# Sums of weight blocks of a retention layer kept in DRAM between two halves of the tokens

## Chip, cores and metric

One core of one Trainium2 chip runs the kernel. The metric is the device time of one execution in microseconds; the kernel before took 1784.6 us (median of 3 runs, 1781.79 to 1789.89).

## What is computed

A two-layer decoder trunk on 1024 tokens of width 1024, all in float32. The part that matters here is the first layer, retention with 4 heads:

```python
u = rms_norm(h, ret_norm_pre[i])
proj = u @ ret_w_in[i]
q, k, v, g = jnp.split(proj, [...], axis=-1)
...
o = retention_chunkwise(q, k, v)
...
o = merge_heads(o).astype(h.dtype) * jax.nn.silu(g)
y = o @ ret_w_out[i]
h = h + rms_norm(y, ret_norm_post[i])
```

For each head, `v` and the gate `g` are 512 columns wide. The second layer is stick-breaking attention with 8 heads, whose keys and values come from a shared projection of the first layer's output.

## The kernel before

**Halves and phases.** The tokens are worked in two halves of 512. `run` (L1179) goes through four phases: retention on the first half (A, t=0), retention on the second (A, t=1), attention on the first half (C, t=0), attention on the second (C, t=1). Weights don't stay on chip: every phase loads them again.

**Products.** A float32 product is made of three products of split operands: `split` (L270) has ScalarE copy the value to a shorter format (the high part) and VectorE subtract that from the value (the low part); `mm3` (L108) multiplies high by high, high by low and low by high. Weights pass through this each time they are loaded: a block of 128 x 512 (256 KB) lands in a `wraw` buffer (6 of them, L42), is split, and stands in a `whl` buffer (3 of them, each for a unit of two blocks).

**The value and gate products (`vg`, L466).** For every head but the first head of the first half, `v` and `g` are computed together by a scheme with seven half-size products in place of eight, at the price of sums of weight blocks. `order` (L524) names the products 1, 2, 5, 6, 3, 7, 4, each in two units `i`. `left(n, i)` (L473) prepares a unit in two blocks `c`: products 1, 2 and 4 take a weight block as it is; product 5 loads two blocks and adds them (L493) into a tile `S` (2 buffers, one for each `i`); product 6 loads one block and changes `S` in place by a subtraction (L496); product 3 loads one block and subtracts `S` from it in its `wraw` buffer (L499); product 7 loads one block and changes `S` in place again (L502). Then comes the split. A head loads 32 blocks. `get(at)` and `get(at + 1)` in `chunk` (L527) ask for the unit in use and the next one. A unit is 12 matmuls on TensorE.

**Heads and their surroundings.** The first head of the first half (u=0, t=0) computes `v` and `g` without this scheme. Between two `vg` stretches stand the query/key products of the next head and the output product of the last one, whose partial sums go to DRAM and back (`y_d`). In the second half `a_post` (L684) rebuilds the first half's residual in side steps (L706, L707, L715 and L716) spread over the heads.

**The order of the work.** All DMAs are issued on SP's queue (`dma`, L63); an issue waits on SP for what its transfer needs. The code only says which instruction needs which: in what order an engine or a queue takes its instructions is laid out beforehand by a planner, so instructions that are ready early can stand ahead of ones written before them. Buffers come free when their last reader is done, a DMA that reads them included.

**A relative of the change that exists already.** In the attention phases the sums of the value weights are made beside other work by `w_sums` (L783, called for t=0), stored to DRAM tiles `S_d` (L289), and loaded in `values` instead of the blocks.

Of the kernel before, what the change touches and what calls it, by code (L numbers as in the profile page):

```python
# [10 lines left out]
F32 = mybir.dt.float32  # L11
# [7 lines left out]
NH = 4  # L19
# [12 lines left out]
def trunk(ctx, tc, xT, wts, gains, trig, ident_in, cols, out):  # L32
# [13 lines left out]
    def S(tag, shape, dt=F32):  # L46
        cnt[0] += 1
        return sb.tile([128] + list(shape), dt, tag=tag, name=f"{tag}{cnt[0]}", bufs=BUFS[tag])

    def PS(tag):  # L50
        cnt[0] += 1
        return ps.tile([128, 512], F32, tag=tag, name=f"p{tag}{cnt[0]}", bufs=BUFS[tag])

    def DRAM(name, dt):
        return dr.tile([128, 1024], dt, tag=name, name=name)
# [4 lines left out]
    def f32(ap):  # L60
        return ap.bitcast(F32)

    def dma(dst, src, eng=nc.sync):  # L63
        eng.dma_start(dst.bitcast(F32), src.bitcast(F32))
# [43 lines left out]
    def mm3(p, lh, ll, rh, rl, start, stop, goes_on=False):  # L108

        kw = dict(skip_group_check=True) if goes_on else {}  # L110
        MM(p, lh, rh, start=start, stop=False, **kw)  # L111
        MM(p, lh, rl, start=False, stop=False, **kw)  # L112
        MM(p, ll, rh, start=False, stop=stop, **kw)  # L113
# [29 lines left out]
    def ahead(n, make):  # L143

        box = {}

        def get(u):
            if u < n and u not in box:
                box[u] = make(u)
            return box.get(u)  # L150
        return get
# [118 lines left out]
    def split(dst, src, scale=None):  # L270

        if scale is None:
            A_.activation(dst[0], src, AF.Copy)  # L273
            V.tensor_tensor(dst[1], src, f32(dst[0]), ALU.subtract)  # L274
        else:
            A_.activation(dst[0], src, AF.Copy, scale=scale)  # L276
            V.scalar_tensor_tensor(dst[1], src, scale, f32(dst[0]), ALU.mult, ALU.subtract)  # L277
# [6 lines left out]
    y_d = [[dr.tile([128, 512], F32, tag=f"y{t}{c}", name=f"y{t}{c}") for c in range(8)] for t in range(2)]  # L284
    h_d = [[DRAM(f"h{t}{c}", F32) for c in range(4)] for t in range(2)]
    k_d = [DRAM(f"k{h}", F32R) for h in range(8)]
    v_d = [[DRAM(f"v{p}{b}", F32R) for b in range(4)] for p in range(NPAIR)]
    T_d = [{n: [DRAM(f"T{t}{n}{i}", F32R) for i in range(2)] for n in (5, 6, 7, 4)} for t in range(2)]
    S_d = [{n: [dr.tile([128, 512], F32, tag=f"s{g}{n}{k}", name=f"s{g}{n}{k}") for k in range(4)]  # L289
# [132 lines left out]
    class AHead:  # L422
# [43 lines left out]
        def vg(self):  # L466


            X, base, h = self.X, self.base, self.h
            self.v, self.sg = [None] * 4, [None] * 4  # L470
            box = {"S": [None, None]}

            def left(n, i):  # L473

                w = S("whl", [2, 1024], F32R)
                if n == 5:
                    box["S"][i] = S("S", [1024])
                for c in range(2):
                    cl = slice(512 * c, 512 * c + 512)

                    def load(which, kk):
                        raw = S("wraw", [512])
                        dma(raw[:], wts[base + 4 + 4 * which + kk, :, cl])
                        return raw[:]

                    s = box["S"][i][:, cl] if box["S"][i] else None
                    if n == 1:
                        src = load(0, i)
                    elif n == 2:
                        src = load(0, 2 + i)  # L490
                    elif n == 5:
                        a, b, src = load(1, i), load(1, 2 + i), s
                        V.tensor_tensor(src, a, b, ALU.add)  # L493
                    elif n == 6:
                        a, src = load(0, i), s
                        V.tensor_tensor(src, src, a, ALU.subtract)  # L496
                    elif n == 3:
                        src = load(0, 2 + i)
                        V.tensor_tensor(src, src, s, ALU.subtract)  # L499
                    elif n == 7:  # L500
                        a, src = load(1, 2 + i), s
                        V.tensor_tensor(src, a, src, ALU.subtract)  # L502
                    else:
                        src = load(1, 2 + i)
                    split((w[:, 0, cl], w[:, 1, cl]), src)
                return w

            def right(n, kt, tb):
                tl = slice(128 * tb, 128 * tb + 128)
                if n in (1, 2, 3):  # L510
                    x, o = X.xh[kt + (0 if n == 1 else 4)], 0 if n == 3 else 256
                    return [x[:, l, o + 128 * tb:o + 128 * tb + 128] for l in range(2)]
                return [X.T[kt][{5: 0, 6: 1, 7: 2, 4: 3}[n]][:, l, tl] for l in range(2)]

            def copy(p):
                c = S("f2", [512])
                A_.activation(c[:], p[:], AF.Copy)
                return c

            def plus(c, p):  # L520
                V.tensor_tensor(c[:], p[:], c[:], ALU.add)
                return c[:]

            order = [(n, i) for n in (1, 2, 5, 6, 3, 7, 4) for i in range(2)]  # L524
            get = ahead(14, lambda at: left(*order[at]))

            def chunk(n, i, kk):  # L527
                if kk == 0:
                    at = order.index((n, i))
                    get(at)  # L530
                    get(at + 1)
                    box["w"] = get(at)
                    if i == 0:
                        first = {1: "ma", 2: "o", 5: "mb", 4: "mb"}.get(n)
                        if first:
                            box["p", n] = [PS(first), PS(first)]
                w, kt = box["w"], 2 * i + kk
                banks = box["p", {6: 1, 7: 1, 3: 5}.get(n, n)]
                first = n in (1, 2, 5, 4)
                for tb in range(2):  # L540
                    xh, xl = right(n, kt, tb)
                    cl = slice(512 * kk, 512 * kk + 512)
                    mm3(banks[tb][:], xh, xl, w[:, 0, cl], w[:, 1, cl], first and kt == 0, kt == 3, goes_on=not first)
                if kt < 3:
                    return
                for tb, p in enumerate(banks):
                    if n in (1, 5, 6, 7):
                        box[n, tb] = copy(p)
                    if n in (1, 5, 6):
                        pass  # L550
                    elif n == 2:
                        self.vput(2 + tb, plus(box[1, tb], p), cc[:, 4 * h + 2 + tb:4 * h + 3 + tb])
                    elif n == 3:
                        self.vput(tb, plus(box[6, tb], p), cc[:, 4 * h + tb:4 * h + tb + 1])
                    elif n == 7:
                        self.gput(tb, plus(box[5, tb], p))
                    else:
                        self.gput(2 + tb, plus(box[7, tb], p))

            return Chunks([lambda n=n, i=i, kk=kk: chunk(n, i, kk) for n, i in order for kk in range(2)], lambda: get(0))  # L560
# [781 lines left out]
```

## Time and profile before

| | us |
|---|---|
| median of 3 runs | 1784.6 |
| lowest and highest run | 1781.79, 1789.89 |
| the profiled execution | 1780.48 |
| its span, first to last instruction | 1778.8 |
| granted TensorE clock, mean | 0.994 |

| engine | busy us | share of the span |
|---|---|---|
| TensorE (PE) | 1719.9 | 97% |
| VectorE (DVE) | 1295.9 | 73% |
| ScalarE (ACT) | 873.0 | 49% |
| GpSimd (POOL) | 285.2 | 16% |

The profile is one execution. PEld is the loading of the stationary operand, which overlaps PE. Rows of the timeline give the start in us from the span's start, the duration, the engine, the line, the operation, the tiles as out<-in, and in brackets the idle time of the engine before it and what ended it. Rows of the waits give the total, the number of waits and the longest. Rows of the windows give, for a stretch of time, each engine's busy time with its count of instructions, the granted clock, the busy share of the 16 DMA engines and the GB/s. A matmul's end is modelled, so PE's busy time hides short pauses. The DMA queue of SP carries all data: 347.26 MB in the execution, 273.78 MB read from DRAM and 73.40 MB written, 57.3% of the engines' time.

### The profile page before, as it was taken

Reading aid. Unit: us, or ns where it says so; the run is one execution under the profiler, and the core shown is the slowest. Engines: PE = TensorE matmul, PEld = TensorE weight load, DVE = VectorE, ACT = ScalarE, POOL = GpSimd, SP = SyncE. Lnnn points to the kernel's source line nnn. Section 1 sums busy time; section 2 is a strip of 40 time slices with the busy share of each in tenths; the row PEclk is TensorE's granted clock in tenths of the full one; section 3 lists DMA queues with packets and bytes.
Section 4 is the critical chain, followed back from the end, with each engine's and each line's share of the span. In section 5 each row is a group of like instructions: output and inputs, shape, how many; then the busy total and the mean of one; then the engine's idle time right before and its main releaser. Section 6 shows DMA issues by size and latency. Waiting matters only on the chain. (4 is left out here: it accounts for less than half of the span.)

```text
span 1778.8 us, 24255 instructions
## 1 busy us (share of the span) xinstructions
PE 1719.9 (97%) x8036; PEld 1416.6 (80%) x8036; DVE 1295.9 (73%) x2131; ACT 873.0 (49%) x1630; POOL 285.2 (16%) x377
## 2 busy tenths in 40 slices
PE   8999999999999899999999999999999999999997
PEld 7888788778788787778777788888887888888776
DVE  7756767889867968597688767668887656757765
ACT  6435545455444535365555444545564444545541
POOL 0210412332304310202112100000200010000003
PEclk9999999999999999999999999999999999999998
DMA  5225465557436656275886888558683762552523
GB/s 191 84 101 196 154 237 172 201 184 272 161 135 208 210 167 214 92 264 188 289 297 225 307 300 292 202 189 283 239 294 109 237 212 97 169 187 95 196 78 118
DMA packets 182381, 348.80 MB, mean 196 GB/s; under 512 B 20336, under 2 KB 24560, under 8 KB 182256
## 3 DMA queue, kind: packets, MB, share of 16 engines
q1 hardware_dynamic: 182256, 347.26, 57.3%
q8 instruction: 63, 1.03, 0.2%
q14 instruction: 62, 0.51, 0.1%
HBM read 273.78 MB, written 73.40 MB: 195 GB/s over the span
## 5 line engine op out<-in xcount | busy, mean ns | idle before, releaser
L274 DVE TENSOR_TENSOR whl<-wraw,whl 128x512 fp32r<-128x512 f32 x368 | 257.7, 730 | 62.8 <-ACT whl L273 62.5
L273 ACT ACTIVATE whl<-wraw 128x512 fp32r<-128x512 f32 x368 | 216.7, 624 | 123.5 <-PE pmb L113 57.3
L276 ACT ACTIVATE whl<-wraw,gn 128x256 fp32r<-128x256 f32 (+1 forms) x240 | 133.5, 605 | 112.4 <-PE pmb L113 58.1
L277 DVE SCALAR_TENSOR_TENSOR whl<-wraw,gn,whl 128x256 fp32r<-128x256 f32 (+1 forms) x240 | 140.4, 625 | 51.1 <-ACT whl L276 47.8
L111 PE MATMUL pmb<-xh,whl 128*128 128x512 f32 x384 | 153.6, 400 | 1.5 <-DVE sg L988 1.4
L111 PE MATMUL pma<-xh,whl 128*128 128x512 f32 x384 | 153.4, 400 | 0.0
L113 PE MATMUL pma<-xh,whl 128*128 128x512 f32 x384 | 150.8, 393 | 0.0
L113 PE MATMUL pmb<-xh,whl 128*128 128x512 f32 x384 | 150.3, 391 | 0.0
L112 PE MATMUL pma<-xh,whl 128*128 128x512 f32 x384 | 150.1, 391 | 0.0
L112 PE MATMUL pmb<-xh,whl 128*128 128x512 f32 x384 | 150.1, 391 | 0.0
L1018 POOL TENSOR_SCALAR_AFFINE_SELECT sgn<-sgn 128x128 f32<-128x128 f32 x64 | 28.2, 441 | 666.4 <-ACT sgn L1013 612.8
L1020 DVE TENSOR_TENSOR_SCAN sgn<-sgn 128x128 f32<-128x128 f32 (+3 forms) x64 | 89.0, 1391 | 28.0 <-POOL sgn L1018 27.9
L273 ACT ACTIVATE AT<-pz 128x512 fp32r<-128x512 f32 (+1 forms) x96 | 46.6, 487 | 118.6 <-PE pz L1050 118.6
L111 PE MATMUL pmb<-oT,whl 128*128 128x512 f32 x240 | 96.7, 403 | 5.9 <-DVE sg L988 3.0
L113 PE MATMUL pmb<-oT,whl 128*128 128x512 f32 x240 | 95.1, 396 | 0.4 <-DVE whl L274 0.4
L274 DVE TENSOR_TENSOR AT<-pz,AT 128x512 fp32r<-128x512 f32 (+1 forms) x96 | 53.0, 554 | 58.2 <-ACT AT L273 57.9
L112 PE MATMUL pmb<-oT,whl 128*128 128x512 f32 x240 | 94.6, 394 | 0.0
L111 PEld LDWEIGHTS pmb<-xh,whl 128*128 128x128 f32 x384 | 72.6, 189 | 17.4 <-DVE sg L988 4.0
L113 PEld LDWEIGHTS pmb<-xh,whl 128*128 128x128 f32 x384 | 72.3, 188 | 15.9
L113 PEld LDWEIGHTS pma<-xh,whl 128*128 128x128 f32 x384 | 72.4, 188 | 15.6
L273 ACT ACTIVATE whl<-S 128x512 fp32r<-128x512 f32 x92 | 56.9, 630 | 56.7 <-DVE S L496 17.0
L112 PEld LDWEIGHTS pmb<-xh,whl 128*128 128x128 f32 x384 | 72.5, 189 | 13.5
(365 smaller groups left out, 4545.8 us busy)
## 6 DMA issues: line engine op xcount, KB each, us to landing
wraw<-in_wts_dram SPq DMA_DIRECT2D x632, 256.0 KB, 3.5
y<-f SPq DMA_DIRECT2D x120, 256.0 KB, 3.1
f<-y SPq DMA_DIRECT2D x88, 256.0 KB, 3.3
wraw<-s SPq DMA_DIRECT2D x48, 256.0 KB, 3.0
T<-AT SPq DMA_DIRECT2D x32, 256.0 KB, 3.0
sc<-T SPq DMA_DIRECT2D x16, 512.0 KB, 4.4
v<-v SPq DMA_DIRECT2D x16, 512.0 KB, 5.1
vo<-v SPq DMA_DIRECT2D x32, 256.0 KB, 2.9
```

Source lines behind the costliest of these rows:

```text
L111: MM(p, lh, rh, start=start, stop=False, **kw)
L112: MM(p, lh, rl, start=False, stop=False, **kw)
L113: MM(p, ll, rh, start=False, stop=stop, **kw)
L273: A_.activation(dst[0], src, AF.Copy)
L274: V.tensor_tensor(dst[1], src, f32(dst[0]), ALU.subtract)
L276: A_.activation(dst[0], src, AF.Copy, scale=scale)
L277: V.scalar_tensor_tensor(dst[1], src, scale, f32(dst[0]), ALU.mult, ALU.subtract)
L1018: G.affine_select(n[:, dg], n[:, dg], [[-1, 128]], ALU.is_gt, 1.0, base=0, channel_multiplier=1)
L1020: V.tensor_tensor_scan(n[:, :W][:, ::-1], n[:, :W][:, ::-1], n[:, :W][:, ::-1], 1.0, ALU.mult, ALU.bypass)
```

## The change

Heads 1, 2 and 3 of the first half store each block that they split for products 5, 6, 3 and 7 to new DRAM tiles `s_d`: 16 blocks a head. For products 5, 6 and 7 the stored block lies in `S`, for product 3 in the `wraw` buffer. In the second half these heads load the 16 blocks from there and split them; they make no sums and take no `S` tile. Products 1, 2 and 4 stay as they were, and so does the first head in the second half, which has no stored blocks (`h` is 0). The tiles of `s_d` for h=1 and product 7 (place 3 in the list) bear the names s130 and s131, which two tiles of `S_d` have as well.

```diff
@@ -284,6 +284,7 @@
     y_d = [[dr.tile([128, 512], F32, tag=f"y{t}{c}", name=f"y{t}{c}") for c in range(8)] for t in range(2)]
     h_d = [[DRAM(f"h{t}{c}", F32) for c in range(4)] for t in range(2)]
     k_d = [DRAM(f"k{h}", F32R) for h in range(8)]
+    s_d = [[[DRAM(f"s{h}{n}{i}", F32) for i in range(2)] for n in range(4)] for h in range(NH)]
     v_d = [[DRAM(f"v{p}{b}", F32R) for b in range(4)] for p in range(NPAIR)]
@@ -473,6 +474,14 @@
             def left(n, i):
 
                 w = S("whl", [2, 1024], F32R)
+                kept = s_d[h][(5, 6, 3, 7).index(n)][i] if n in (5, 6, 3, 7) and h else None
+                if kept is not None and self.t:
+                    for c in range(2):
+                        cl = slice(512 * c, 512 * c + 512)
+                        raw = S("wraw", [512])
+                        dma(raw[:], kept[:, cl])
+                        split((w[:, 0, cl], w[:, 1, cl]), raw[:])
+                    return w
                 if n == 5:
                     box["S"][i] = S("S", [1024])
                 for c in range(2):
@@ -503,6 +512,8 @@
                     else:
                         src = load(1, 2 + i)
                     split((w[:, 0, cl], w[:, 1, cl]), src)
+                    if kept is not None:
+                        dma(kept[:, cl], src)
                 return w
```

## The prediction

> **What bounds the kernel now.** I read the page first (busy time, then the DMA issues), then the table of windows over the stretches that the change touches, then the waits and the order of time inside one of them.
>
> ```profile
> span 1778.8 us, 24255 instructions
> PE 1719.9 (97%) x8036; PEld 1416.6 (80%) x8036; DVE 1295.9 (73%) x2131; ACT 873.0 (49%) x1630; POOL 285.2 (16%) x377
> wraw<-in_wts_dram SPq DMA_DIRECT2D x632, 256.0 KB, 3.5
> y<-f SPq DMA_DIRECT2D x120, 256.0 KB, 3.1
> f<-y SPq DMA_DIRECT2D x88, 256.0 KB, 3.3
> wraw<-s SPq DMA_DIRECT2D x48, 256.0 KB, 3.0
> S<-in_wts_dram SPq DMA_DIRECT2D x16, 256.0 KB, 5.3
> s<-S SPq DMA_DIRECT2D x16, 256.0 KB, 4.4
> ```
>
> TensorE is the bound: outside 1778.8 - 1719.9 = 59 us it always has a product running. A helper engine or a transfer matters only where it makes PE wait, so the change is worth what it does to PE's idle time in six stretches: the value-and-gate products (`vg`) of heads 1, 2 and 3, in the first token half (sums are made, and will be written) and in the second (they will be loaded). The windows view gives one row for each, in that order:
>
> ```profile
> core 0: us, PE busy (x) PEld busy (x) DVE busy (x) ACT busy (x) POOL busy (x), PEclk, DMA share, GB/s
> 147.00:186.00 39.00, 39.00 (x174) 32.27 (x173) 34.69 (x59) 24.77 (x43) 1.76 (x2) 1.00 0.60 197
> 252.00:290.50 38.50, 38.50 (x171) 31.85 (x171) 34.91 (x60) 24.36 (x42) 1.85 (x2) 1.00 0.60 200
> 351.00:382.00 31.00, 29.46 (x138) 23.48 (x138) 28.52 (x50) 20.59 (x38) 12.32 (x4) 1.00 0.57 185
> 565.00:612.00 47.00, 41.94 (x179) 32.83 (x178) 41.25 (x60) 27.13 (x49) 14.19 (x11) 1.00 0.74 254
> 671.00:714.00 43.00, 42.04 (x188) 34.13 (x187) 36.35 (x63) 24.17 (x42) 2.66 (x5) 1.00 0.61 198
> 764.00:803.00 39.00, 38.20 (x172) 30.85 (x171) 36.20 (x61) 24.08 (x44) 2.97 (x5) 1.00 0.79 267
> ```
>
> The reader is to see three things. PE idles 0, 0 and 1.5 us in the first half and 5.1, 1.0 and 0.8 us in the second: 6.8 us is what the second half can give back inside these stretches. VectorE is busy some 90% of each. And DMA is at 0.6 of its engines, so there is room, but not twice the room. The first row also gives PE's pace: 39.00 / 174 = 0.224 us a product, 12 products a unit, 2.69 us a unit.
>
> **What the second half gains.** For each of three heads the sums 5, 6, 3 and 7 are no longer computed: 4 x 4 = 16 subtractions or additions a head. Their group rows:
>
> ```profile
> L493 DVE TENSOR_TENSOR S<-wraw,wraw 128x512 f32<-128x512 f32 x28 | 22.2, 796 | 24.8 <-DMA wraw<-in_wts_dram 24.7
> L496 DVE TENSOR_TENSOR S<-S,wraw 128x512 f32<-128x512 f32 x28 | 18.7, 699 | 1.7 <-DMA wraw<-in_wts_dram 1.7
> L499 DVE TENSOR_TENSOR wraw<-wraw,S 128x512 f32<-128x512 f32 x28 | 18.9, 691 | 0.0
> L502 DVE TENSOR_TENSOR S<-wraw,S 128x512 f32<-128x512 f32 x28 | 19.0, 683 | 1.3 <-DMA wraw<-in_wts_dram 1.3
> L273 ACT ACTIVATE whl<-S 128x512 fp32r<-128x512 f32 x92 | 56.9, 630 | 56.7 <-DVE S L496 17.0 <-DVE S L493 14.0 <-PE po L113 7.6
> ```
>
> In the four DVE rows 78.8 us stand in 112 instructions; 48 go, so about 34 us of VectorE, 11 us a head. Unit 5 loads one kept sum where it loaded two blocks: 4 loads fewer a head, 12 in all; 16 of a head's 28 loads then come from DRAM sums (3.0 us to landing against 3.5, no worse). VectorE's 34 us lie beside PE, which is busy; only PE's waits count. For the worst head the wait view of 565 to 613 us says what they are:
>
> ```profile
> PE pma L111 <- ACT whl L273: 1.7, 2, 0.9
> PE pma L112 <- DVE whl L274: 1.5, 2, 0.9
> PE pmb L112 <- DVE whl L274: 1.3, 1, 1.3
> PE po L112 <- DVE whl L274: 0.5, 1, 0.5
> ```
>
> All are waits for the split of a weight unit, which VectorE does behind its sums. Not all go. One of the two waits in each of the first two rows, some 1.6 us together, falls right behind these two, where ScalarE stood in another step and VectorE waited for it:
>
> ```profile
> 586.90 0.63 ACT L715 ACTIVATE vo<-vo 128x512 f32<-128x512 f32 x1 [2.32 <-POOL vo L707]
> 588.08 1.35 DVE L274 TENSOR_TENSOR whl<-S,whl 128x512 fp32r<-128x512 f32 x1 [2.36 <-ACT whl L273]
> ```
>
> That is the residual of the first half being rebuilt (L707, L715), which the change does not touch. The gain lies between 0 and 6.8 us; I take two thirds, **4.5 us**. What is late next is that step, and nothing new.
>
> **What the first half pays.** 3 heads x 4 sums x 2 x 2 = 48 stores of 256 KB on SP's queue, no compute instruction. Net transfers: +48 - 12 = +36. Price of one, from a stretch where stores and loads of this size run dense (the sums of the attention weights):
>
> ```profile
> 1000.00:1010.00 10.00, 10.00 (x46) 8.32 (x46) 6.63 (x11) 4.56 (x9) 0.90 (x2) 1.00 0.95 334
> ```
>
> 334 GB/s for 10 us is 12.7 transfers of 262,144 bytes in 9.5 busy us: 0.75 us each, and PE idles nothing at 0.95. In head 1 the share goes from 0.60 x 39 = 23.4 us to 23.4 + 16 x 0.75 = 35.4 us, 0.91; in head 3's window from 17.7 to 29.7 of 31 us, 0.96. So it fits, with nothing left over. Total DMA is not the cost; lateness of single loads is. The order of time in head 1, and under it a window's row of the time from unit 6 on:
>
> ```profile
> 146.75 0.69 DVE L493 TENSOR_TENSOR S<-wraw,wraw 128x512 f32<-128x512 f32 x1 [3.29 <-DMA wraw<-in_wts_dram]
> 151.41 0.69 DVE L493 TENSOR_TENSOR S<-wraw,wraw 128x512 f32<-128x512 f32 x1 [1.38 <-DMA wraw<-in_wts_dram]
> 157.53 0.69 DVE L496 TENSOR_TENSOR S<-S,wraw 128x512 f32<-128x512 f32 x1 [0.81 <-DMA wraw<-in_wts_dram]
> 163.67 1.29 DVE L496 TENSOR_TENSOR S<-S,wraw 128x512 f32<-128x512 f32 x2
> 164.87 0.68 DVE L499 TENSOR_TENSOR wraw<-wraw,S 128x512 f32<-128x512 f32 x1
> 165.47 1.36 DVE L274 TENSOR_TENSOR whl<-S,whl 128x512 fp32r<-128x512 f32 x2
> 172.17 0.69 DVE L274 TENSOR_TENSOR whl<-S,whl 128x512 fp32r<-128x512 f32 x1
> 174.56 0.39 PE L111 MATMUL pma<-whl,A 128*128 128x512 f32 x1
> 158.00:181.00 23.00, 23.00 (x103) 19.05 (x102) 22.90 (x39) 15.26 (x27) 0.00 (x0) 1.00 0.54 185
> ```
>
> Up to 157.5 us VectorE waits for loads; from there to 181 it works without a pause (DVE 22.90 of 23 us). The four stores of unit 5 now stand in the queue ahead of loads that VectorE waits for: 4 x 0.75 = 3.0 us. That shift is carried to the end of the stretch. Slack there: unit 7's first split ends at 172.17 + 0.69 = 172.86, PE takes it up at 174.56, so 1.7 us. PE loses 3.0 - 1.7 = 1.3 us in heads 1 and 2; head 3, which idles already, has no slack and loses 3.0. Sum 1.3 + 1.3 + 3.0 = **5.6 us**, between 0 (the queue's gaps swallow the stores, as at 1000 us) and the 21 us of the slower rival.
>
> Two new waits cost nothing in this sum. The sum in `S` is overwritten by the next one (L496, L502), which must now wait until the store has read it: 157.53 - 147.44 = 10 us lie between, and the store lands in 3 to 4.4. Queued behind the store on SP are the next weight loads. SP waits there for the same instructions already (its waits from 142 to 187 us):
>
> ```profile
> SPq L64 <- DVE whl L274: 15.9, 17, 3.3
> SPq L64 <- DVE S L496: 6.1, 4, 3.9
> SPq L64 <- DVE S L493: 5.3, 4, 2.0
> ```
>
> That is 27 of 45 us for a free `wraw` buffer, which comes from the sum or the split behind it; a store that waits for the same sum holds up no load that could have gone earlier, if stores are issued where their data is due.
>
> The Trainium skill, DMA: Bandwidth & Descriptors, section "Anatomy of one DMA — SWDGE (gpsimd) path", says that most of a transfer's fixed time is the wait for the target memory's confirmation of the write, worst when that is HBM; by it stores would land later than loads and hold their buffers longer, which would point to the slower rival below. Here they do not: y<-f lands in 3.1 us and f<-y in 3.3.
>
> **Rivals.** *Slower: buffers turn too slowly.* Units 5, 6, 3 and 7 need 20 loads in 8 x 2.69 = 21.5 us, so each of six buffers must come round in 6.45 us. Now it takes 3.2 to 3.5 to land and 0.69 + 0.63 + 0.69 = 2.0 for sum, ScalarE half (L273) and VectorE half. The rival decides where a load lands in over 4.45 us; in the dense stretch they took 5.3 (S<-in_wts_dram above). Then a turn takes 7.3, and 20 x 7.3 / 6 = 24.3, 2.8 us late, and the four buffers of unit 3 stay taken for their stores (4.4 us, s<-S above): 4 x 4.4 / 6 = 2.9 more. 5.7 a head: 4.0 behind the slack of 1.7, 7.0 with the shift of 3.0 on top. Three heads at 5.7 are 17, less the gain of 4.5: +12.6, **1797**; three at 7.0 and no gain: +21, 1806. Against it: at 0.6 share there are gaps to fill, and PE has 1.7 us in hand.
>
> *Slower by far: written order.* If SP followed the order in which the code is written, load, sum, store would run one after the other: 16 x (3.2 + 0.69) = 62 us a head where PE takes 21.5, with 158 - 147 = 11 us in hand: 29.5 x 3 = 88, less 4.5: 1868. The rows speak against it: at 163.67 to 165.47 two differences of unit 6 and one of unit 3 run ahead of unit 6's splits, which are written between them. Each engine's order comes from a planner by readiness.
>
> *Faster.* The stores cost nothing and all idle time comes back. By PE's pace it is a little more than the busy column says: 179, 188 and 172 products want 40.1, 42.1 and 38.5 us of 47, 43 and 39, which leaves 8.3. And with 34 us taken from VectorE head 3's rotary products, which PE awaits ahead of the stretch, come sooner:
>
> ```profile
> PEld pz L113 <- DVE qk L274: 1.9, 2, 1.3
> ```
>
> 8.3 + 1.9 = 10.2: 1774. Against it: the row at 586.90.
>
> *Not as said.* Two kept tensors bear the same names (s130, s131) as sums of the attention weights and would share a place in DRAM. The former are last read in the window that ends at 803 us, the latter written in the stretch at 1000; a wait there would be over: 1785.
>
> **How the numbers follow.** The profiled execution: 1780.5 with a span of 1778.8. -4.5 + 5.6 = +1.1 us, 1781.6 on that basis; the median of the runs is 1784.6, 4.1 us above, so **1786** (1784.6 + 1.1, rounded). Half a per cent, about what a measurement here can tell from no change, is 8.9 us. Chances: forecast 0.48 (own range 1777 to 1793), not as said 0.01, faster 0.14, buffers 0.34, written order 0.03. So faster 0.14, same 0.49, slower 0.37. Range: from the faster case, 1774, to the end of the buffer case, 1806; outside remain written order and the tails.
>
> **What would show it.** Right: issues s<-S x52 (16 before), s<-wraw x12, wraw<-s x96 (48 before), wraw<-in_wts_dram x572, L493 x16, VectorE near 1262 us; PE idle in the second-half stretches down to some 2 us, in the first half up by 1 to 3 a head; DMA share there near 0.9. The buffer rival: wraw landing over 4.45 us in these stretches, VectorE idle for DMA past 160 us, PE idle of 5 us or more a head. Written order: stores and loads strictly alternating on SP. I would be wrong if the planner lays out other steps anew, since then PE idles where nothing was changed.

## The result and the profile after

Six runs each: 1796.17 us after (1791.34 to 1802.11), 1783.28 us before (1781.62 to 1789.89). The ratio is 1.0064 [1.005, 1.0078], some 11.4 us: **slower by 0.64%**. (A ratio here is an estimate over all runs, not the quotient of the two medians, which differ by 12.9 us; in the experiments below the two ways differ by up to 2.3 us.) The profiled execution took 1791.34 us, its span is 1789.6 us against 1778.8, its mean granted clock 0.991 against 0.994. The likeliest case of the prediction was no change that can be measured, at 1786 (1777 to 1793), and the result lies outside that; the range over all its cases went from 1774 to 1806. The result lies where the buffer rival had it, at 1797, but not for that rival's reason, as the runs below show: that the wide range holds it is luck.

The page of the changed kernel, its busy times and the DMA issues that answer to those quoted of before:

```profile
span 1789.6 us, 24277 instructions
...
PE 1723.3 (96%) x8036; PEld 1418.2 (79%) x8036; DVE 1266.6 (71%) x2083; ACT 869.1 (49%) x1630; POOL 277.4 (16%) x377
...
wraw<-in_wts_dram SPq DMA_DIRECT2D x572, 256.0 KB, 3.7
...
wraw<-s SPq DMA_DIRECT2D x96, 256.0 KB, 3.3
...
s<-S SPq DMA_DIRECT2D x52, 256.0 KB, 3.3
```

The change is there as said: 48 sums gone (x2131 to x2083 on VectorE, 29.3 us less busy), 60 weight loads fewer, 48 loads of sums more, 36 stores from `S` (and 12 from `wraw`). PE computes the same 8036 products, 10.8 us later. The windows of the same stretches (three in the first half, three in the second; they lie later now, so the borders are moved):

```profile
core 0: us, PE busy (x) PEld busy (x) DVE busy (x) ACT busy (x) POOL busy (x), PEclk, DMA share, GB/s
146.50:187.00 40.50, 39.88 (x176) 32.49 (x175) 33.35 (x55) 24.59 (x43) 0.45 (x1) 1.00 0.90 292
255.00:297.00 42.00, 39.94 (x174) 31.98 (x173) 34.94 (x58) 24.20 (x42) 1.33 (x3) 1.00 0.87 289
357.50:393.00 35.50, 31.51 (x147) 25.35 (x147) 30.00 (x51) 20.61 (x38) 6.89 (x4) 1.00 0.90 288
577.50:625.00 47.50, 43.11 (x174) 34.05 (x173) 33.29 (x47) 25.90 (x48) 15.49 (x12) 0.93 0.80 261
683.50:728.00 44.50, 44.50 (x203) 36.98 (x202) 29.84 (x50) 26.35 (x47) 2.74 (x5) 1.00 0.57 185
775.00:814.00 39.00, 36.97 (x169) 30.21 (x168) 32.64 (x52) 30.70 (x56) 5.37 (x4) 1.00 0.64 209
```

PE's idle time is what to read (length less PE busy): 0.6, 2.1 and 4.0 us in the first half, where before had 0, 0 and 1.5, and 4.4, 0 and 2.0 us in the second, where it had 5.1, 1.0 and 0.8. So the first half pays, and the second, whose VectorE now rests, gives back almost nothing.

When the same product starts in both traces shows where PE falls behind (each pair is the start of one run of products on PE in the two timelines):

| place | before, us | after, us | PE is late by |
|---|---|---|---|
| head 1, end of `vg` | 180.7 | 181.2 | 0.5 |
| its output product | 214.6 | 218.3 | 3.7 |
| head 2, end of `vg` | 285.2 | 291.9 | 6.7 |
| head 3, end of `vg` | 390.4 | 400.4 | 10.0 |
| first half, end of it | 402.1 | 410.1 | 8.1 |
| second half, head 1 | 576.8 | 589.4 | 12.6 |
| | 590.7 | 599.6 | 8.8 |
| | 597.5 | 612.7 | 15.2 |
| head 3 | 779.7 | 790.0 | 10.3 |
| near the end | 1679.0 | 1689.4 | 10.5 |

The delay of 8 to 10 us is there at 400 us, before the first kept sum is loaded. What PE waited for, in the wait view of 142 to 410 us; first before, then after:

```profile
PE pz L679 <- DVE oT L274: 3.0, 2, 1.6
...
PE pma L112 <- DVE whl L274: 0.8, 1, 0.8
PE pmb L112 <- DVE small L632: 0.7, 1, 0.7
PE pma L111 <- DVE small L632: 0.5, 1, 0.5
```

```profile
PE pz L690 <- DVE oT L274: 4.5, 2, 3.0
PE pmb L112 <- DVE small L643: 2.1, 1, 2.1
PE pmb L112 <- DVE whl L274: 1.9, 1, 1.9
PE pma L112 <- DVE whl L274: 1.8, 3, 0.9
...
PE pma L111 <- ACT whl L273: 0.9, 1, 0.9
```

Waits for split weights (`whl`) grow from 0.8 to 4.6 us, waits for the steps of the head's output on VectorE (`oT`, `small`) from 4.2 to 6.6. Most of the rest of the way to 8.1 us is a period of a slower TensorE clock behind such a wait, which costs 1.7 us (last section). Of the step from 8.1 to 12.6 a stop of 1.9 us at 449.5 us and the slower period behind it make 3.6. That stop (PE waits for L213, a step of the output product) lies between the two halves' `vg` stretches, in work that the change does not touch.

### The profile page after: what moved, and what is told of

Read it like the earlier page. It is cut to its first block, busy times and chain, and to the rows that moved or that the text cites. A ratio compares the mean times of both kernels' runs of the same rounds, so it can differ in the third digit from the quotient of the medians.

```text
span 1789.6 us, 24277 instructions
## 1 busy us (share of the span) xinstructions
PE 1723.3 (96%) x8036; PEld 1418.2 (79%) x8036; DVE 1266.6 (71%) x2083; ACT 869.1 (49%) x1630; POOL 277.4 (16%) x377
## 4 chain that ended last, share of the span: by engine, by line
PE 27%; issue 19%; DVE 7%; DMA 3%; POOL 1%; ACT 1%; SPq 0%; POOLq 0%; DVEq 0%; ACTq 0%
PE pmb L112 4%; PE pmb L113 4%; PE pmb L111 4%; PE pma L111 3%; PE pma L112 3%; PE pma L113 3%; PE po L112 1%; PE po L113 1%; PE po L111 1%; DVE sgn L1031 1%; DVE whl L277 1%; DMA S<-y 1%; PE pz L1061 1%; DMA wraw<-in_wts_dram 1%; POOL sgn L1029 1%
## 5 line engine op out<-in xcount | busy, mean ns | idle before, releaser
L274 DVE TENSOR_TENSOR whl<-wraw,whl 128x512 fp32r<-128x512 f32 x404 | 281.6, 727 | 82.3 <-ACT whl L273 81.5
L273 ACT ACTIVATE whl<-wraw 128x512 fp32r<-128x512 f32 x404 | 236.8, 624 | 135.7 <-PE pmb L113 53.3
L113 PEld LDWEIGHTS pma<-xh,whl 128*128 128x128 f32 x384 | 72.4, 189 | 15.8
L111 PEld LDWEIGHTS pma<-xh,whl 128*128 128x128 f32 x384 | 72.6, 189 | 14.0 <-DVE sg L999 1.1
```

## The experiments

**The theories.** *Place in the queue*: SP issues its transfers one after the other; a store waits there for its sum, and weight loads whose buffer is free stand behind it, issue late and land late. *Bytes*: 48 transfers of 256 KB more make every load slower. *Buffers*: stores hold `S` and `wraw`, so sums and loads wait for their landing (the buffer rival). *Plan*: with the stores in the program the planner lays the order of the other instructions out anew. *The second half* has a theory of its own: its gain is there and the residual step of head 1 eats it. All differences are to the kernel before, run on the same chip beside the experiment, with the 95% interval of the ratio; the microseconds are worked out from the ratio.

**1. The stores alone.** The second half makes its own sums again.

```diff
-                if kept is not None and self.t:
+                if False:
...
-                    if kept is not None:
+                    if kept is not None and not self.t:
                         dma(kept[:, cl], src)
```

> The first half stores its 48 blocks as in the change; the second half makes its sums itself, as before, and reads nothing of them. Theory of late loads (the bytes of the stores delay the weight loads that VectorE waits for in the three first-half stretches, and PE pauses of 2 us and more are followed by a period at half clock): +8 to +12 us, since TensorE in the changed kernel is 10.0 us behind at 390 us. Theory of the plan (the order laid out by the planner moved, and the stores are cheap in themselves): no sign is fixed, anything from -3 to +12. My forecast's own term: +5.6.

Measured: 1796.98 against 1784.42, 1.007 [1.0045, 1.0095], +12.5 us. The stores alone cost what the whole change does (8.0 to 17.0 us against 8.9 to 13.9). In its profiled execution, of 1800.0 us, PE is 12.5 us late at the end of the first half (414.1 us) and 18.8 us at 595.6 us, where nothing is changed, so not all of the cost arises where the stores stand.

**2. The loads alone.** No stores; each kept load reads one weight block instead, so VectorE and the number of transfers in the second half are as in the change.

```diff
-                        dma(raw[:], kept[:, cl])
+                        dma(raw[:], wts[base + 4 + 4 * (n in (5, 7)) + (2 * (n in (3, 7)) + i), :, cl])
...
-                    if kept is not None:
-                        dma(kept[:, cl], src)
```

> Nothing is stored, and in the second half heads 1 to 3 load one plain weight block in place of each kept sum, with no sums made: the arithmetic of the sums is left out, the transfers and instructions of the second half are those of the change. My forecast's term: -4.5 us (between 0 and -6.8). If the residual step (L726 on ScalarE waits for a GpSimd addition that waits for a load) and the half-clock periods behind it take the gain: -1 to +2, with a ScalarE wait of 5 us before such a step in head 1. If the lost gain was only a consequence of the first half's lateness: -5 to -10.

Measured: 1779.66, 0.997 [0.9954, 0.9986], -5.3 us. The forecast gain of 4.5 us exists where nothing is paid ahead of it. The kernel leaves out the arithmetic of the sums, so its output is not the layer's.

**3. The waits with few bytes.** Every store of kernel 1 carries two columns, 1 KB in all.

```diff
-                        dma(kept[:, cl], src)
+                        dma(kept[:, 512 * c:512 * c + 2], src[:, 0:2])
```

> As the stores-only kernel, but each of the 48 stores moves 2 columns of the block instead of 512 (128 x 8 bytes); the second half makes its sums itself. All waits and queue places of the stores stay, the bytes go. Late loads: 0, within 3 us of before. Held buffers (sums and load buffers stay taken until a store has landed, about 2 us even for a small one): +4 to +8. Plan: as the stores-only kernel, within 3 us of it.

Measured: 1788.49, 1.0022 [1.0009, 1.0036], +3.9 us (1.6 to 6.4). Even almost without bytes the stores cost time, about a third of the whole. They still hold their buffers, and land in 2.4 us; kernels 4 and 12 look at that part.

**4. Product 3's sum out of the load buffers.** The whole change, with the sum of product 3 written to a `ko` tile, so that its store holds no `wraw` buffer.

```diff
-                        src = load(0, 2 + i)
-                        V.tensor_tensor(src, src, s, ALU.subtract)
+                        a = src = load(0, 2 + i)
+                        if kept is not None:
+                            if c == 0:
+                                box["K"] = S("ko", [1024])
+                            src = box["K"][:, cl]
+                        V.tensor_tensor(src, a, s, ALU.subtract)
```

> The whole change, but in the first half product 3's sum goes to a buffer of its own (tag ko) and is stored from there, so that its load buffer comes free after the subtraction and not after the landing of the store. Held buffers: at most +6 us against before, where the change has +11. Late loads: still +9 to +12. My slower rival gave the held buffers 2.9 us of 5.7 a head, so by it +4 to +8.

Measured: 1791.82, 1.0054 [1.0038, 1.007], +9.6 us: as slow as the change, within the intervals. Load buffers held by product 3's stores are not the main cause; the interval, 6.8 to 12.5 us, leaves room for a smaller part.

**5. The stores on another queue.** Kernel 1 with the stores issued by GpSimd, so that no load stands behind one.

```diff
-                        dma(kept[:, cl], src)
+                        dma(kept[:, cl], src, G)
```

> As the stores-only kernel (+12.5 us against before), but the 48 stores are issued by GpSimd instead of SP: the same bytes, no place in SP's queue. Late loads by bytes on the shared DMA engines: still +8 to +13. Late loads by places in SP's queue (an issue that waits for a sum holds up the loads behind it): +1 to +5. A GpSimd that is held by the issues would show as longer waits for its additions and powers, and could add some us of its own.

Measured: 1804.73 against 1782.11, 1.0114 [1.0087, 1.0141], +20 us: slower still and outside both expectations, so this way out is none. SP's own waits from 142 to 192 us and the landing of the stores from `S` in this kernel show what is new:

```profile
SPq L64 <- DMA s<-wraw: 6.3, 2, 6.0
```

```profile
s<-S POOLq DMA_DIRECT2D x36, 256.0 KB, 4.9
```

From GpSimd the stores of `S` land in 4.9 us (3.4 in kernel 1, in a row that holds 16 of the attention's too), those of `wraw` in 3.9 us (3.8), and a load waits up to 6.0 us for a buffer that a store still reads. Here the buffer rival's mechanism does act. So this run put another cost in the place of the one taken away, and doesn't tell whether the place on SP's queue was it.

**6. Half the bytes.** Kernel 1 with 256 of each 512 columns stored.

```diff
-                        dma(kept[:, cl], src)
+                        dma(kept[:, 512 * c:512 * c + 256], src[:, 0:256])
```

> As the stores-only kernel, with half of each block's columns stored (128 x 256). Full stores gave +12.5, stores of 2 columns +3.9. By bytes the middle: +8, between +6 and +10. If only the step from a small to a landing of several us matters: near +12. If the full stores' cost was mostly the plan's order: no order, within 0 to +13.

Measured: 1791.98, 1.0064 [1.0046, 1.0083], +11.4 us, not told apart from all the bytes. A cost in proportion to the bytes, between 3.9 and 12.5, would have been 8.2; its ratio, 1.0046, is the lower end of the interval.

**7. Product 5 alone.** Only the sums of product 5, the one that needs two blocks, are kept: 12 stores. The second half loads them into `S`, and the other sums are made from there.

Against the kernel before:

```diff
+                kept = s_d[h][(5, 6, 3, 7).index(n)][i] if n == 5 and h else None
...
+                    elif n == 5 and kept is not None and self.t:
+                        src = s
+                        dma(src, kept[:, cl])
...
+                    if kept is not None and not self.t:
+                        dma(kept[:, cl], src)
```

> Only product 5's sums are kept: 12 stores instead of 48 in the first half; in the second half heads 1 to 3 load them into S, saving 12 loads and 12 additions, and make the other sums as before. By bytes the stores cost 12.5 / 4 = 3 us; the gain is a part of the 5.3 us that the loads-only kernel gave, 2 to 4, since the additions of product 5 are those that wait for loads. Net -1 to +2. If the gain hangs on the 36 other differences too, +2 to +4.

Measured: 1779.36, 0.9976 [0.9966, 0.9985], -4.3 us (-6.1 to -2.7): **faster than both kernels**, and better than expected. The windows of the second half, with the borders that the prediction showed for before:

```profile
core 0: us, PE busy (x) PEld busy (x) DVE busy (x) ACT busy (x) POOL busy (x), PEclk, DMA share, GB/s
565.00:612.00 47.00, 45.24 (x191) 34.96 (x190) 38.69 (x58) 26.23 (x49) 15.07 (x11) 1.00 0.70 237
671.00:714.00 43.00, 43.00 (x195) 35.73 (x194) 36.51 (x62) 25.84 (x46) 2.33 (x4) 1.00 0.55 178
764.00:803.00 39.00, 38.44 (x175) 31.45 (x174) 37.48 (x62) 24.42 (x45) 9.10 (x6) 1.00 0.62 203
```

PE idles 1.8, 0 and 0.6 us where it idled 5.1, 1.0 and 0.8, and VectorE is about as busy as before. At the end of the first half PE is where it was before (0.2 us earlier).

**8. The residual's loads ahead of their step.** The whole change; the side steps of the first half's residual load one piece ahead.

```diff
-        return [stat1, stat2, row] + in_turn(8, 1 if t else 0, load, add, square) + [stat3]
+        return [stat1, stat2, row] + in_turn(8, 1, load, add, square) + [stat3]
```

> The whole change, and the residual step of the second half loads its two blocks one step ahead (lead 1 instead of 0). If ScalarE's wait for this step (5.46 us before L726 in head 1) and the half-clock period behind it ate the second half's gain: 4 to 7 us faster than the change, so +4 to +7 against before. If not: within 2 us of the change's +11.

Measured: 1798.33, 1.0084 [1.0065, 1.0102], +15 us. A miss: no gain comes back. But the edit did not take the wait away that it was aimed at. In head 1 of the second half ScalarE still waits for this step; in the wait views, first the change (577 to 625 us), then this kernel (577 to 628):

```profile
ACT vo L726 <- POOL vo L718: 18.1, 6, 5.5
```

```profile
ACT vo L726 <- POOL vo L718: 20.7, 6, 5.1
```

So the theory that this step holds the second half's gain is not tested by it and stays open.

**9. All but product 5.** 36 stores, for products 6, 3 and 7.

```diff
-                kept = s_d[h][(5, 6, 3, 7).index(n)][i] if n in (5, 6, 3, 7) and h else None
+                kept = s_d[h][(5, 6, 3, 7).index(n)][i] if n in (6, 3, 7) and h else None
```

> The other part of the change alone: the sums of products 6, 3 and 7 are kept (36 stores) and loaded in the second half, product 5 is summed in both halves from two blocks. If the second half's gain comes from product 5's loads and additions, and the first half's cost from the stores of 6, 3 and 7: +8 to +14 us, with nothing gained back in the second half. If the cost goes by bytes alone: 36/48 of 12.5 = +9, less a gain of 1 to 3. If the 36 differences saved on VectorE are worth something of the loads-only kernel's 5.3: +4 to +7.

Measured: 1794.44 against 1785.03, 1.0057 [1.0036, 1.0078], +10.2 us. By the time alone the cost of the stores and a gain can't be told apart. In the trace PE is 12.2 us late at the end of the first half, as in kernel 1, and 14.5 us at 825 us of the time before: the stores cost about what all 48 do, and the 36 differences that VectorE is spared bring no gain that shows.

**10. The bytes without the waits.** Kernel 1, but each of the 48 stores reads a table that has long been on chip. Same number, size, queue and target; no sum to wait for and no buffer of a sum or a load to hold.

```diff
-                        dma(kept[:, cl], src)
+                        keep(nc.sync.dma_start(kept[:, cl], X.cos[:]))
```

> The second half as before; in the first half 48 stores of 256 KB as in the stores-only kernel, pinned on SP's queue behind the load that is written before them, but of a table that lies ready (the cosines) instead of the sums: the bytes stay, nothing waits for a sum and no sum or load buffer is held for a store. The sums are not what is stored. If the bytes cost (late loads): +7 to +12, as the difference of the stores-only kernel and that with 2 columns (8.6) and up to its whole 12.5. If the waits and held buffers cost: 0 to +4.

Measured: 1785.7, 1.0005 [0.9991, 1.002], +0.9 us (-1.6 to +3.6). **The bytes by themselves cost nothing that shows.** Their traffic is all there. The window of head 1 and the median landing of the stores (`s<-tab`; 8 of the 56 are the attention's):

```profile
146.50:187.00 40.50, 39.86 (x174) 32.06 (x172) 34.64 (x58) 25.25 (x44) 1.25 (x3) 1.00 0.83 287
```

```profile
wraw<-in_wts_dram SPq DMA_DIRECT2D x632, 256.0 KB, 3.8
s<-tab SPq DMA_DIRECT2D x56, 256.0 KB, 5.2
```

287 GB/s against 292 in the change, and the loads land in 3.8 us, which is what they take in kernel 1 too.

**11. Products 5 and 7.** Kernel 7, and product 7's sum kept as well: 24 stores. Against kernel 7:

```diff
-                kept = s_d[h][(5, 6, 3, 7).index(n)][i] if n == 5 and h else None
+                kept = s_d[h][(5, 6, 3, 7).index(n)][i] if n in (5, 7) and h else None
...
+                    elif n == 7 and kept is not None and self.t:
+                        src = S("wraw", [512])[:]
+                        dma(src, kept[:, cl])
```

> As the kernel that keeps only product 5's sums (-4.3 us against before with this one's batch), plus those of product 7, whose sum is the last use of S: 24 stores, and 12 differences fewer on VectorE in the second half. If VectorE's differences are worth nothing there and stores cost by bytes: -4.3 + 12 x 0.18 = about -2, between -4 and 0. If VectorE's time counts: -6 to -8. If stores hurt only from a certain density on: -5 to -3.

Measured: 1782.39, 0.9995 [0.9982, 1.0008], -0.9 us (-3.2 to +1.4). Twelve stores more than in kernel 7, and no gain that is clear of the noise is left; as the intervals of the two overlap, that these stores cost what was gained is likely and not shown.

**12. Two tiles for the sums.** The whole change; sums 5 and 3 in `S`, 6 and 7 in a `ko` tile, so that no sum overwrites one that is still being stored and no store holds a load buffer.

```diff
+                if n == 6 and kept is not None:
+                    box["K", i] = S("ko", [1024])
...
-                        a, src = load(0, i), s
-                        V.tensor_tensor(src, src, a, ALU.subtract)
+                        a, src = load(0, i), s if kept is None else box["K", i][:, cl]
+                        V.tensor_tensor(src, s, a, ALU.subtract)
...
```

> The whole change with the same 48 stores, but the sums alternate between two tiles in the first half: product 5 in S, 6 in a ko tile, 3 in S again, 7 in the ko tile. No sum is overwritten sooner than four units after it is stored (10.8 us; before, product 6 overwrote product 5's two units after), and no load buffer waits for a store to land. Stores still wait on SP's queue for their sums, and the bytes are the same. Held buffers: the first half's cost falls to 0 to 4 us, in all -4 to +3 against before. Places in SP's queue (a store that waits for its sum holds up the loads behind it): still +8 to +12.

Measured: 1793.17 against 1783.27, 1.0057 [1.0035, 1.0079], +10.2 us (6.2 to 14.1). As the main cause, the buffer theory falls with it.

## The wait, read in the trace

Kernels 1 and 10 differ in what a store reads: in kernel 10 it waits for no sum and holds no buffer. The order of time of SP in the changed kernel, in head 1 (a row is a group of issues, its duration runs from the start of the first to the end of the last), and below it VectorE:

```profile
162.90 1.52 SPq L64 DMA_DIRECT2D s<-S  x3
164.47 1.19 SPq L64 DMA_DIRECT2D wraw<-in_wts_dram  x2
166.58 2.31 SPq L64 DMA_DIRECT2D s<-wraw  x3
168.94 1.79 SPq L64 DMA_DIRECT2D wraw<-in_wts_dram  x2
170.82 0.39 SPq L64 DMA_DIRECT2D s<-wraw  x1
```

```profile
162.19 1.89 DVE L505 TENSOR_TENSOR S<-S,wraw 128x512 f32<-128x512 f32 x3
...
165.87 1.89 DVE L508 TENSOR_TENSOR wraw<-wraw,S 128x512 f32<-128x512 f32 x3
...
173.19 1.49 DVE L511 TENSOR_TENSOR S<-wraw,S 128x512 f32<-128x512 f32 x2 [0.63 <-DMA wraw<-in_wts_dram]
```

The last of the three differences L505 ends at 162.19 + 1.89 = 164.08 and sets a `wraw` buffer free. The load that takes it is issued at 168.94, 4.9 us later, behind three stores `s<-wraw`; the first of these could not go before its sum L508, which ends near 165.87 + 1.89/3 = 166.5, and the group takes 2.3 us. The load lands at 173.17, and VectorE, idle for 0.63 us, starts L511 on it at 173.19. In head 1 PE still loses little by this (0.5 us at the end of `vg`). In the trace before, SP's row at this place is one group of loads, with no store in it:

```profile
160.05 20.08 SPq L64 DMA_DIRECT2D wraw<-in_wts_dram  x13
```

In kernel 10 the stores stand just as densely between the loads, but SP passes each within half a microsecond:

```profile
164.02 0.43 SPq L516 DMA_DIRECT2D s<-tab  x1
164.55 0.38 SPq L64 DMA_DIRECT2D wraw<-in_wts_dram  x1
164.97 0.49 SPq L516 DMA_DIRECT2D s<-tab  x1
165.55 0.44 SPq L64 DMA_DIRECT2D wraw<-in_wts_dram  x1
166.04 0.49 SPq L516 DMA_DIRECT2D s<-tab  x1
```

The same for all loads issued from 160 to 183 us, 15 or 16 in each kernel. I joined each load with the last reader of the buffer that it can take and with its own first reader; a release is thus worked out from the order of instructions, the issue and the landing are the trace's:

| mean, us | buffer free to issue | issue to landing | landing to first use | used within 0.3 us of landing |
|---|---|---|---|---|
| before | 0.03 | 2.93 | 3.58 | 0 of 15 |
| kernel 10, bytes only | 0.21 | 3.99 | 2.27 | 0 of 15 |
| kernel 3, waits, 1 KB stores | 1.08 | 3.70 | 1.45 | 6 of 16 |
| kernel 7, product 5 | 0.03 | 3.37 | 2.83 | 0 of 15 |
| the change | 2.15 | 4.38 | 0.54 | 8 of 16 |

A load used to lie ready for 3.6 us before it was read. Bytes take 1.3 us of that, waits with hardly any bytes 2.1; both together take 3.0, and half of the loads are read the moment they land. This would explain why the costs don't simply add up: as long as there is a reserve a late load is nearly free, and once it is used up the lateness reaches VectorE and PE. The same working in heads 2 and 3 gives 2.3 and 2.6 us from free to issue in the change, 0.1 in the kernel before, and 0.3 and 0.8 in kernel 10. Kernel 4 fits: its `wraw` buffers need not wait for a store's landing, yet its loads are issued no sooner (3.18 us after the buffer is free).

## Why the prediction was right or wrong

- **Transfers, counts, VectorE: right.** The counts came as listed, VectorE at 1266.6 us against near 1262 (29.3 us saved, not 34), the DMA share at 0.87 to 0.90 in the first-half stretches. Bytes as such cost +0.9 us (kernel 10), which doesn't show.
- **The step that failed** is the one on the new waits: "a store that waits for the same sum holds up no load that could have gone earlier". It does: loads went 2.15 us after their buffer was free instead of 0.03. I had read SP's 27 us of waits in head 1 as waits that the stores would share. But those waits were for buffers, and a load left as soon as one was free; a store waits for a sum whose operands come later than that. The totals of SP's waits don't show this, since they tell what SP waits for and not what stands behind it.
- **The first-half term, 5.6 us, measured +12.5** (kernel 1; the interval is 8.0 to 17.0). It was built from bytes alone: four stores of unit 5 at 0.75 us, less 1.7 us of slack. Product 5's stores, of all, are the ones that cost nothing that shows (kernel 7: PE 0.2 us earlier at the end of the first half). In the changed kernel's three stretches PE's idle time did grow by 5.2 us (0.6 + 2.1 + 4.0, less 1.5), near the term, but by luck, as it came from other stores; and the term left out what follows outside the stretches, the longer waits for the head's output and the slower clock. The bound of 21 us held.
- **The slack of 1.7 us** was the wrong reserve to look at. It is PE's at the end of the stretch; what was used up was the reserve between the landing of a load and its use.
- **The second-half term, -4.5 us, was right as a size where it stands alone** (kernel 2, -5.3) and not had by the whole change. I took it as two thirds of PE's idle time there, behind all 48 sums; but kernel 7 gets -4.3 with 12 of them, and kernel 9, with the other 36, nothing that shows. What helps seems to be one load and no waiting for two; this reading is by exclusion.
- **"What is late next is that step, and nothing new": half right.** In head 1 of the second half PE goes from 12.6 us late to 8.8 and then to 15.2. ScalarE stood for the residual step:

```profile
600.86 0.63 ACT L726 ACTIVATE vo<-vo 128x512 f32<-128x512 f32 x1 [5.46 <-POOL vo L718]
```

  It waited 5.46 us there (before, not at all at the same step, the fifth, at 602.13 us, and 2.32 us at the fourth), and PE then stopped for 1.9 and 1.1 us. Kernel 8 did not take this wait away and so doesn't decide. Why the whole change doesn't keep kernel 2's gain behind its own stores stays open. By the noise it may keep a part: the sum of kernels 1 and 2 is +7.2 us with several us either way, and the change's +11.4 may be 8.9.
- **The buffer rival** named 1797 and loads landing in over 4.45 us. The tile view of `wraw` gives medians of 4.0, 4.0 and 4.3 us to landing in the three stretches, just short of that. In kernel 10 they are 4.3, 4.2 and 5.1, later still, at a cost of 0.9 us; and kernels 4 and 12 take the held buffers away without a gain. Its number was right for another reason, and was itself loose: it took 5.7 us a head and left out the slack of 1.7 and the shift of 3.0 that stand beside it. Written order and "not as said" did not come.
- **"I would be wrong if the planner lays out other steps anew": it came too, in part.** The stop of 1.9 us at 449.5 us has no counterpart before: in the wait view of 402 to 577 us the kernel before has 1.5 us of waits, all for `whl`. No run holds the order fixed, so what the plan costs by itself stays open. Against it as the main cause: kernel 10 takes its differences L505 three in a row just as the change does (162.93 us) and costs 0.9, and the kernels with 36 or 48 full stores that wait for sums on SP's queue (1, 4, 8, 9, 12 and the change) all cost between 9.6 and 15.
- **Queue or not: how far it is shown.** That the cost comes with the waits and not with the bytes alone is shown by kernels 1, 3 and 10; that it isn't in the main the held buffers, by 4 and 12. That it is the place on SP's queue is what the rows say, but the one run that took the stores off that queue (kernel 5) brought a cost of its own.

## What to carry to other kernels

By these runs a transfer added to a queue that feeds the bound engine is priced by what it waits for, before its bytes: look at what stands behind it, and at how long loads now lie ready before they are read, since that reserve is what it spends. Where a precomputed operand is worth keeping, try first the one that saves a load (here a sum of two blocks) and measure it alone; the rest may cost more than it brings. A wait that goes by another path, such as another engine's queue, has to be measured too: here it was worse.

## What the runs showed of the hardware

TensorE's granted clock falls to half for 3.4 us after a short stop of PE, which the prediction did not reckon with. Three such places of the changed kernel in the windows view (the PEclk is the column after POOL's):

```profile
214.50:218.00 3.50, 3.45 (x11) 2.81 (x12) 3.46 (x6) 0.60 (x1) 0.00 (x0) 0.51 0.65 178
450.00:453.50 3.50, 3.50 (x10) 2.25 (x9) 3.42 (x4) 1.74 (x4) 2.61 (x2) 0.51 0.93 327
603.60:610.40 6.80, 5.74 (x14) 4.48 (x15) 4.42 (x5) 4.31 (x9) 2.01 (x2) 0.50 0.73 221
```

Each follows a stop that the change brought or lengthened. In the timeline of PE the stops ahead of the first and the second (214.55 and 449.51 us), and between them one as long that brought no such period:

```profile
214.55 1.11 PE L690 MATMUL pz<-ident,sgn 128*128 128x128 f32 x4 [3.00 <-DVE oT L274]
...
375.06 0.50 PE L112 MATMUL pmb<-whl,xh 128*128 128x512 f32 x1 [1.90 <-DVE whl L274]
...
449.51 0.50 PE L111 MATMUL pmb<-xh,whl 128*128 128x512 f32 x1 [1.89 <-DVE f L213]
```

A period of 3.4 us at half speed costs 1.7. The changed kernel has four of them more in these places (the last is two), the kernel before one more than it elsewhere (two between 960 and 985 us, against one): net three, about 5 of the 10.8 us. So a stop of 2 us can cost nearly 4, or only 2. The Trainium skill, TensorE: Matmul & The Clock Gate, section "HAM oscillation — how this bites in real kernels", gives the rule that PE should have no idle gaps over some 3.4 us; these were 1.9 to 3.0 us by the trace, so here the rule's threshold is too high. The length of the periods agrees with what its Part 1, "The HAM clock gate", says: activity is judged in a free-running window of 3413 ns. The traces bear a free-running window out. In the changed kernel the slower periods start at 214.50, 450.02, 603.62, 972.26, 1685.64 and 1726.60 us, and each lies a whole number of times 3.413 us behind the first (69, 114, 222, 431 and 443). On this grid the stop ahead of 375.06 us lies across a border, at 374.92 us, and the one ahead of 449.51 us within one window. The windows view of these two:

```profile
371.51:374.92 3.41, 1.66 (x8) 1.04 (x6) 2.52 (x4) 1.74 (x3) 0.00 (x0) 1.00 0.88 312
446.61:450.02 3.41, 1.52 (x7) 0.98 (x6) 3.41 (x8) 1.73 (x3) 0.09 (x1) 1.00 0.87 308
```

PE idles 1.75 us of the first, which passed, and 1.89 us of the second, behind which the clock fell. Over all traces of this case (60 to 1765 us) every window with 1.93 us of idle or more is followed by half the clock, none with less than 1.35 us at full clock is, and between the two it went either way.
